# The decay sums of a state-space scan: which matrix is held and which is moved

## The chip, the cores and the metric

The kernel runs on one core of one Trainium2 chip. The metric is the device time of one execution in microseconds. Three runs of the kernel before took 1081.53, 1081.97 and 1082.54 us; the median is 1081.97 us. The names of the engines are those of the profile: PE is TensorE (matrix products), PEld its loading of the held operand, DVE is VectorE, ACT is ScalarE, POOL is GpSimd, and SP issues most of the DMAs.

## The reference, cut to what matters

The reference is a two-layer encoder over 256 tokens of width 1024. Each layer is a SwiGLU feed-forward block, a token mixer and a second feed-forward block, each followed by a layer norm, with shift, scale and gate computed from a condition vector. One of the two head groups of the mixer is a Mamba-2 scan with 8 heads. The part that the change touches is the decay between two tokens of a chunk:

```
a    = dt * A                                  # one number per token and head
a_cs = cumsum(a)                               # inside a chunk
seg  = a_cs[l] - a_cs[s]                       # sum of a over s < k <= l
decay = exp(where(s <= l, seg, -inf))
y_diag = einsum(C, B, decay, x * dt)
```

The kernel uses chunks of 128 tokens in place of 64, so there are two of them, t = 0 and t = 1. For each chunk and head it needs a 128 x 128 matrix of the sums of a over s < k <= l.

## The kernel before, in words

All weights are f32 in memory. ACT copies each piece into the format fp32r ("high"), DVE subtracts this copy from the original ("low"), and PE forms three products high·high, high·low and low·high. This is the bulk of PE's work. Weights come in pieces of 512 KB through a ring of 9 raw buffers; SP issues a load when a buffer's last reader (on DVE) is done. The pieces of the condition matrix (`ada`) go through the same ring, and DVE multiplies and adds them up without PE.

The high and low copies, and most intermediate tiles of the mixer, share one pool of 26 slots of 4 KB per partition, called `w` (function `wtile`). PSUM tiles of the mixer come from `mps` (two banks), `gps` (two banks) and `apt` (four banks).

The order of the work inside the mixer follows the list `MIX`. It gives the program order and so the priority; the order of the instructions on each engine is then fixed at build time by a list scheduler with a cost model of its own, which lets a later operation go first where an earlier one isn't ready in its reckoning. On the chip each engine runs its instructions in this fixed order. Only in the crossing from one block to the next is the order written out by hand. In every profile line the operations on PE, DVE and ACT carry L105, the line of the recording helper, so they are told apart by tile names. An x in a name stands for the mixer.

The steps of `MIX` around the change, in their order, are: `xe 0` and `xe 1` (the causal convolution of x: ACT `ca`, three steps on DVE, ACT `th`, DVE `xcx`, four times), `am t` (function `seg_pre`), `st` (one piece of the stream), `v 0` (24 x 2 products `ov`), `ta 0` (transposes `paT`), `seg t` (products `pse`, then `mt` = exp), `sg t` (DVE: `mt` times the matrix `gm`), `tx t` (transposes `pxs` of x), `v 1`, `av`, `y t` (products `pd`), `z 0`, `z 1` (products `oz`), then the output projection `p` (products `acc`, weights `w2`, `w3`, `w0`, `w1`).

The decay sums: `tri[k, l]` is 1 where l >= k, and `gtm[k, s]` is 1 where k > s. For each head ACT scales `gtm` by the column of a (`am`, eight activations of 128 x 128 for one t), and PE forms the product of the held `am` and the moved `tri` into a quarter of a PSUM bank; four heads fill a bank, and one ACT instruction takes the exponential of the whole bank. Both operands are f32.

Of the kernel before, what the change touches and what calls it, by code (L numbers as in the profile page):

```python
# [11 lines left out]
F32 = mybir.dt.float32  # L12
F32R = mybir.dt.float32r
BF16 = mybir.dt.bfloat16
I32 = mybir.dt.int32
AF = mybir.ActivationFunctionType
# [4 lines left out]
P = 128  # L21
# [11 lines left out]
HEADS = 8  # L33
# [33 lines left out]
def kernel(  # L67
# [24 lines left out]
    G = nc.gpsimd  # L92
# [19 lines left out]
    V, S, PE = Queue(nc.vector), Queue(nc.scalar), Queue(nc.tensor)  # L112
# [9 lines left out]
    cp = ctx.enter_context(tc.tile_pool(name="cp", bufs=1))  # L122
# [4 lines left out]
    sm = ctx.enter_context(tc.tile_pool(name="sm", bufs=3))  # L127
# [4 lines left out]
    def wtile(shape, name, dt=F32):  # L132
        return wp.tile([P] + list(shape), dt, tag="w", name=name)

    def mps(name):
        return pms.tile([P, 512], F32, tag="ms", name=name)
# [10 lines left out]
    def f(ap):  # L147
        return ap.bitcast(F32)
# [6 lines left out]
    def split(src, hi, lo):  # L155
        S.copy(hi, src)
        V.tensor_tensor(lo, src, f(hi), op=ALU.subtract)
# [6 lines left out]
    tri = cp.tile([P, P], F32, name="tri")  # L164
    G.affine_select(out=tri, in_=ones, compare_op=ALU.is_ge, fill=0.0, base=0,
                    pattern=[[1, P]], channel_multiplier=-1)
    gtm = cp.tile([P, P], F32, name="gtm")
    G.affine_select(out=gtm, in_=ones, compare_op=ALU.is_gt, fill=0.0, base=0,
                    pattern=[[-1, P]], channel_multiplier=1)
    neghalf = cp.tile([P, 16], F32, name="neghalf")  # L170
    G.memset(neghalf, -0.5)

# [781 lines left out]
    def mixer(mx_, nxt):  # L954
        l, qk, nm = mx_.l, mx_.qk, mx_.nm
# [69 lines left out]
        aa = sm.tile(bcs, F32, tag="aa", name="aa" + nm, bufs=1)  # L1025
# [180 lines left out]
        ssd = {}  # L1206

        def seg_pre(t):
            am = wtile([HEADS, P], f"am{nm}_{t}")
            for h in range(HEADS):  # L1210
                S.activation(am[:, h, :], gtm, AF.Identity, scale=aa[:, t, h:h + 1])
            ssd[t] = am

        def seg(t):
            am = ssd[t]
            mt = wtile([HEADS, P], f"mt{nm}_{t}")
            for g in range(2):
                ps = mps(f"pse{nm}_{t}{g}")
                for h in range(4):
                    PE.matmul(ps[:, h * P:(h + 1) * P], lhsT=am[:, 4 * g + h, :], rhs=tri, start=True, stop=True)  # L1220
                S.activation(mt[:, 4 * g:4 * g + 4, :], ps.rearrange("p (h k) -> p h k", h=4), AF.Exp)
            ssd[t] = mt

# [83 lines left out]
        def v_copy(t):  # L1307
# [3 lines left out]
        ops = dict(qk=mx_.proj, ev=mx_.evac, small=small, rope=rope, tqk=turn_qk, st=step,  # L1311
                   dt=lambda: held.update(dt=dt_mm()), dtf=lambda: dt_finish(*held.pop("dt")),
                   xm=xbc_mm, xe=xbc_evac, sc=scores_mm, sm=softmax, cums=cums, gram=gram, am=seg_pre,
                   cb=combine, ta=turn_a, seg=seg, sg=seg_mul, v=lambda t: tok_mm("v", t), vc=v_copy, tx=turn_x,
                   y=y_mm, av=lambda t: av(t, vt), z=lambda t: tok_mm("z", t), carry=carry, flush=flush,
                   gz=gate_z, pre=lambda: step(PRE), tf=to_feature, p=proj, up=upto_, rows=lambda: held.update(rows=ln_rows(l, s)))
# [9 lines left out]
    for l in range(DEPTH):  # L1326
        m, g = ms[l], gs[l]
# [41 lines left out]
```

## Time and profile before

| what | value |
|---|---|
| median of 3 runs | 1081.97 us |
| the profiled execution | 1082.18 us |
| its span, first to last instruction | 1080.3 us |
| mean granted TensorE clock | 0.984 |
| instructions on PE | 7433 |

The profile is one execution; its span is the time between the first and the last instruction, and the profiled execution took 1.88 us more than that. The granted clock is given in parts of full speed. Rows of a timeline give the start in us, the duration in us, the engine, and what is written from what; "[idle before <-releaser]" is the time that the engine stood idle before the instruction and what ended it. Matmuls are pipelined: the duration of one is longer than the distance between the starts of two, and it is the distance that counts for a sum.

### The profile page before, as it was taken

Reading aid. Unit: us, or ns where it says so; the run is one execution under the profiler, and the core shown is the slowest. Engines: PE = TensorE matmul, PEld = TensorE weight load, DVE = VectorE, ACT = ScalarE, POOL = GpSimd, SP = SyncE. Lnnn points to the kernel's source line nnn. Section 1 sums busy time; section 2 is a strip of 40 time slices with the busy share of each in tenths; the row PEclk is TensorE's granted clock in tenths of the full one; section 3 lists DMA queues with packets and bytes.
Section 4 is the critical chain, followed back from the end, with each engine's and each line's share of the span. In section 5 each row is a group of like instructions: output and inputs, shape, how many; then the busy total and the mean of one; then the engine's idle time right before and its main releaser. Section 6 shows DMA issues by size and latency. Waiting matters only on the chain.

```text
span 1080.3 us, 18994 instructions
## 1 busy us (share of the span) xinstructions
PE 1035.6 (96%) x7433; PEld 950.9 (88%) x7433; DVE 835.1 (77%) x1310; ACT 553.1 (51%) x946; POOL 53.0 (5%) x93
## 2 busy tenths in 40 slices
PE   4999999999997999999999999999999989999996
PEld 2799999989895899999988999998989979999995
DVE  5788688689988898769489768856999888756454
ACT  3475344476654664434466434546566567435241
POOL 1000000020010200000010000000100120000000
PEclk8999999999998999999999999999999999999999
DMA  9989888838368398789637889784664738776411
GB/s 343 311 301 383 292 291 313 295 114 270 100 202 281 120 307 306 293 323 328 237 117 259 302 317 362 277 288 126 174 212 141 230 101 304 247 241 214 161 40 39
DMA packets 162557, 258.24 MB, mean 239 GB/s; under 512 B 10806, under 2 KB 125982, under 8 KB 162468
## 3 DMA queue, kind: packets, MB, share of 16 engines
q1 hardware_dynamic: 162468, 257.04, 69.4%
q8 instruction: 58, 0.95, 0.3%
q14 instruction: 31, 0.25, 0.1%
HBM read 255.96 MB, written 1.05 MB: 238 GB/s over the span
## 4 chain that ended last, share of the span: by engine, by line
PE 77%; DVE 11%; ACT 6%; DMA 2%; issue 2%; POOL 1%; SPq 0%; DVEq 0%; POOLq 0%; ACTq 0%
PE ob L105 37%; PE acc L105 18%; PE oa L105 6%; PE oqkx L105 5%; PE accx L105 3%; PE ocx L105 2%; DVE xs L105 1%; PE ovx L105 1%; DVE ada L105 1%; DVE acc L105 1%; DVE cax L105 1%; PE pr L105 1%; ACT um L105 1%; ACT junk L105 1%; DVE lu L105 1%
## 5 line engine op out<-in xcount | busy, mean ns | idle before, releaser
L105 PE MATMUL ob<-uH,hg 128*128 128x256 f32 x576 | 163.1, 283 | 0.0
L105 PE MATMUL ob<-uL,hg 128*128 128x256 f32 x576 | 162.4, 282 | 0.0
L105 PE MATMUL ob<-uH,lg 128*128 128x256 f32 x576 | 161.8, 281 | 0.0
L105 PE MATMUL ob<-uH,hu 128*128 128x256 f32 x576 | 161.7, 281 | 0.0
L105 PE MATMUL ob<-uH,lu 128*128 128x256 f32 x576 | 161.7, 281 | 0.0
L105 PE MATMUL ob<-uL,hu 128*128 128x256 f32 x576 | 161.7, 281 | 0.0
L105 PE MATMUL acc<-ho,hH 128*128 128x512 f32 x352 | 137.5, 392 | 0.2 <-ACT hH L105 0.2
L105 PE MATMUL acc<-lo,hH 128*128 128x512 f32 x352 | 137.3, 390 | 0.0
L105 PE MATMUL acc<-ho,hL 128*128 128x512 f32 x352 | 137.2, 391 | 0.0
L105 ACT ACTIVATE sgb<-ob 128x256 f32<-128x256 f32 x72 | 27.6, 383 | 213.9 <-PE ob L105 213.3
L105 DVE TENSOR_TENSOR lo<-raw_o,ho 128x1024 fp32r<-128x1024 f32 x88 | 105.9, 1221 | 13.4 <-PE ob L105 6.5
L105 PEld LDWEIGHTS ob<-uH,hg 128*128 128x128 f32 x576 | 108.3, 188 | 7.8 <-issue 3.7
L105 PEld LDWEIGHTS ob<-uH,lg 128*128 128x128 f32 x576 | 110.2, 191 | 0.1
L105 PEld LDWEIGHTS ob<-uL,hg 128*128 128x128 f32 x576 | 108.2, 188 | 2.3
L105 PEld LDWEIGHTS ob<-uH,lu 128*128 128x128 f32 x576 | 110.2, 191 | 0.0
L105 DVE TENSOR_TENSOR lg<-raw_g,hg 128x1024 fp32r<-128x1024 f32 x84 | 100.6, 1221 | 11.5 <-ACT hg L105 6.1
L105 PEld LDWEIGHTS ob<-uH,hu 128*128 128x128 f32 x576 | 108.5, 188 | 0.0
L105 PEld LDWEIGHTS ob<-uL,hu 128*128 128x128 f32 x576 | 108.1, 188 | 0.0
L105 DVE TENSOR_TENSOR hfb<-ob,sgb 128x256 f32<-128x256 f32 x72 | 30.4, 422 | 94.4 <-ACT sgb L105 94.2
L105 DVE TENSOR_TENSOR lu<-raw_u,hu 128x1024 fp32r<-128x1024 f32 x84 | 100.6, 1220 | 3.5 <-ACT hu L105 1.9
L105 ACT CAST hg<-raw_g 128x1024 fp32r<-128x1024 f32 x84 | 86.3, 1050 | 32.0 <-PE acc L105 18.2
L105 ACT CAST ho<-raw_o 128x1024 fp32r<-128x1024 f32 x88 | 90.2, 1049 | 10.5 <-PE ob L105 9.0
(537 smaller groups left out, 2263.5 us busy)
## 6 DMA issues: line engine op xcount, KB each, us to landing
raw_o<-in_w_ffn_out_dram SPq DMA_DIRECT2D x88, 512.0 KB, 6.0
raw_g<-in_w_ffn_in_dram SPq DMA_DIRECT2D x84, 512.0 KB, 5.7
raw_u<-in_w_ffn_in_dram SPq DMA_DIRECT2D x84, 512.0 KB, 5.9
raw<-in_w_ffn_in_dram SPq DMA_DIRECT2D x8, 512.0 KB, 8.1
lg<-in_ln_g_dram SPq DMA_DIRECT2D x6, 512.0 KB, 6.2
lb<-in_ln_b_dram SPq DMA_DIRECT2D x6, 512.0 KB
raw_qk0x<-in_w_in_dram SPq DMA_DIRECT2D x4, 512.0 KB, 7.8
raw_qk1x<-in_w_in_dram SPq DMA_DIRECT2D x4, 512.0 KB
```

Of the source, the lines that this page charges most:

```text
L105: ins = emit(*args, **kwargs)
```

## The change

The roles of the two matrices are exchanged. The constant `gtm`, in an fp32r copy `gtmr` made once at the start on POOL, is now the held operand. The scaled matrix is now `tri` times a; it is made twice, from the high and the low part of a, as fp32r, and it is the moved operand. Since the held operand is the same for all heads, one product takes four heads (512 columns) at a time, and two products (high, low) add up in one bank. The column of a is split by one ACT copy and one DVE subtraction per t. There are now sixteen activations per t, and two tiles of the pool `w` where there was one.

```diff
+    gtmr = cp.tile([P, P], F32R, name="gtmr")
+    G.tensor_copy(gtmr, gtm)
...
         def seg_pre(t):
-            am = wtile([HEADS, P], f"am{nm}_{t}")
+            ssd[t] = am = [wtile([HEADS, P], f"am{e}{nm}_{t}", F32R) for e in "hl"]
+            ah = sm.tile([P, HEADS], F32R, tag="ah", name=f"ah{nm}_{t}", bufs=2)
+            al = sm.tile([P, HEADS], F32, tag="al", name=f"al{nm}_{t}", bufs=2)
+            split(aa[:, t, :], ah, al)
             for h in range(HEADS):
-                S.activation(am[:, h, :], gtm, AF.Identity, scale=aa[:, t, h:h + 1])
-            ssd[t] = am
+                S.activation(am[0][:, h, :], tri, AF.Identity, scale=f(ah)[:, h:h + 1])
+                S.activation(am[1][:, h, :], tri, AF.Identity, scale=al[:, h:h + 1])

         def seg(t):
...
-                for h in range(4):
-                    PE.matmul(ps[:, h * P:(h + 1) * P], lhsT=am[:, 4 * g + h, :], rhs=tri, start=True, stop=True)
+                for e in range(2):
+                    PE.matmul(ps, lhsT=gtmr, rhs=am[e][:, 4 * g:4 * g + 4, :], start=(e == 0), stop=(e == 1))
                 S.activation(mt[:, 4 * g:4 * g + 4, :], ps.rearrange("p (h k) -> p h k", h=4), AF.Exp)
```

## Rows read from the trace of the kernel before

**Rows 1.** The page's first part: busy us, share of the span, instructions of three engines.

```profile
PE 1035.6 (96%) x7433; PEld 950.9 (88%) x7433; DVE 835.1 (77%) x1310; ACT 553.1 (51%) x946; POOL 53.0 (5%) x93
```

**Rows 2.** Stretches (start:end, length, busy us by engine, clock), layer 0 then 1.

```profile
318.00:345.00 27.00, 20.33 (x120) 15.72 (x119) 22.62 (x32) 11.51 (x29) 4.16 (x3) 0.81 0.84 286
822.00:838.00 16.00, 15.71 (x135) 15.26 (x134) 14.99 (x24) 11.41 (x31) 0.68 (x1) 1.00 0.64 210
838.00:879.00 41.00, 40.58 (x252) 34.94 (x251) 35.08 (x62) 22.98 (x46) 4.85 (x10) 1.00 0.61 197
```

**Rows 3.** Timeline of PE in layer 1, the decay sums of t = 1.

```profile
830.94 1.12 PE L105 MATMUL psex<-tri,amx 128*128 128x128 f32 x8
831.82 0.36 PE L105 MATMUL ovx<-hv1x,uH 128*128 128x256 f32 x1
...
832.25 1.05 PE L105 MATMUL psex<-tri,amx 128*128 128x128 f32 x8
833.15 0.60 PE L105 MATMUL paTx<-ident,prx 128*128 128x128 f32 x4
833.50 0.36 PE L105 MATMUL ozx<-hz0x,uH 128*128 128x256 f32 x1
```

**Rows 4.** Timeline of PE in layer 1, two fp32r products of 512 columns.

```profile
853.28 0.39 PE L105 MATMUL accx<-lw2x,uH 128*128 128x512 f32 x1
853.51 0.40 PE L105 MATMUL accx<-hw2x,uH 128*128 128x512 f32 x1
```

**Rows 5.** Timeline of ACT in layer 1, around the scaled matrices.

```profile
814.88 2.16 ACT L105 ACTIVATE amx<-gtm,aax 128x128 f32<-128x128 f32 x7 [0.44 <-PE ocx L105]
...
817.55 0.55 ACT L105 ACTIVATE cax<-ocx,cvx 128x256 f32<-128x256 f32 x1
822.26 0.42 ACT L105 ACTIVATE thx<-cax 128x256 f32<-128x256 f32 x1 [4.16 <-DVE cax L105]
...
827.36 0.42 ACT L105 ACTIVATE thx<-cax 128x256 f32<-128x256 f32 x1 [1.91 <-DVE cax L105]
827.68 2.44 ACT L105 ACTIVATE amx<-gtm,aax 128x128 f32<-128x128 f32 x8
832.10 0.60 ACT L105 ACTIVATE mtx<-psex 128x512 f32<-128x512 f32 x1 [1.98 <-PE psex L105]
```

**Rows 6.** Timeline of PE in layer 0, after the decay sums.

```profile
326.25 2.07 PE L105 MATMUL pdx<-xdx,mtx 128*128 128x64 f32 x16 [1.88 <-DVE yc11x L105]
...
332.71 1.08 PE L105 MATMUL pr<-ada,ones 128*32 128x256 f32 x8 [3.00 <-DVE uL L105]
...
335.16 0.63 PE L105 MATMUL accx<-lw2x,uH 128*128 128x512 f32 x1
335.59 0.63 PE L105 MATMUL accx<-hw2x,uL 128*128 128x512 f32 x1
```

**Rows 7.** Timeline of DVE in layer 0, the stream.

```profile
307.63 1.28 DVE L105 SCALAR_TENSOR_TENSOR ada<-raw_(0, 5, 3)_1_3208,cT,ada 128x1024 f32<-128x1024 f32 x1
...
315.28 1.23 DVE L105 TENSOR_TENSOR lw2x<-raw_w2x,hw2x 128x1024 fp32r<-128x1024 f32 x1 [1.45 <-ACT hw2x L105]
```

**Rows 8.** Timeline of SP, the load that follows.

```profile
308.94 3.92 SPq L203 DMA_DIRECT2D raw_w2x<-in_w_out_dram  x2
```

**Rows 9.** Groups by form: names, shapes, count, busy us, mean ns, idle before.

```profile
L105 PE MATMUL psex<-tri,amx 128*128 128x128 f32 x64 | 8.8, 280 | 0.5 <-ACT aTx L105 0.5
L105 ACT ACTIVATE amx<-gtm,aax 128x128 f32<-128x128 f32 x32 | 10.0, 388 | 0.8 <-PE ocx L105 0.8
L105 DVE SCALAR_TENSOR_TENSOR ddx<-ddx,dz2x 128x16 f32<-128x16 f32 x14 | 2.4, 169 | 0.1
L168 POOL TENSOR_SCALAR_AFFINE_SELECT gtm<-ones 128x128 f32<-128x128 f32 x1 | 0.3, 292 | 0.0
```

**Rows 10.** Stretch of half clock in layer 0 (columns as in rows 2).

```profile
328.00:338.00 10.00, 7.00 (x24) 4.50 (x23) 10.00 (x11) 2.12 (x3) 0.00 (x0) 0.50 0.90 298
```

## The prediction, made before the changed kernel ran

> **What bounds the kernel now.** I read the shares of the engines first: PE is busy 96% of the span, DVE 77%, ACT 51% [rows 1]. That says PE bounds the whole; it doesn't say that PE bounds the stretch of the change. So I read the two mixers by stretches. In layer 1 PE is busy for 15.71 of 16 us while the decay sums are made, and for 40.58 of 41 us from there to the end of the output projection, at full clock [rows 2]. There PE's own work is the path: what it saves early, it has at the end. In layer 0 the stretch after the decay sums looks different: PE is busy 20.33 of 27 us at a mean clock of 0.81, DVE 22.62 [rows 2]. PE waits 1.88 us and 3.00 us there, both times for DVE [rows 6]. DVE is held in turn by the stream of weights: the last piece of one condition chunk is used up at 307.63 + 1.28 us, SP can then issue the load of w2 at 308.94, and DVE stands idle for 1.45 us before the first piece of w2 at 315.28 [rows 7, 8]. So in layer 0 a lead of PE ends in a longer wait for DVE. The same step of the same mixer is worth something in one layer and little in the other.
>
> **PE: what goes and what comes.** The 64 psex instructions of the trace are 32 f32 products (2 chunks, 2 layers, 8 heads), each recorded as two [rows 9]. Their 8.8 us of busy time is not the price, since they overlap; the distance of starts is. The group at 830.94 gives way to the next operation at 831.82, the one at 832.25 at 833.15: 0.88 and 0.90 us for four heads [rows 3]. Eight groups cost 8 x 0.89 = 7.1 us. In their place come two fp32r products of 512 columns per group. The trace has that form in accx: starts at 853.28 and 853.51, 0.23 us apart [rows 4]. Eight groups at 2 x 0.23 = 0.46 us cost 3.7 us. PE saves 7.1 - 3.7 = 3.4 us, 1.7 us in each layer. Bounds: a lone product shows 0.39 us [rows 4], so a group may take 0.23 + 0.39 = 0.62 us and PE save only 2.2 us in all; at best the products vanish behind others and the saving is the whole 7.1 us. I take 3.4 us, because the accx rows are the same form, back to back.
>
> The Trainium skill has other prices for a stream of products ("TensorE: Matmul & The Clock Gate", Back-to-back issue gap): about 81 ns for 128 columns and 131 ns for 512, sustained. By these a group would go from 0.65 to 0.26 us and PE would save 3.1 us. The rows say 0.11 and 0.23 us for the two forms, so here the trace differs, and it decides.
>
> **ACT: sixteen activations for eight.** One am takes 388 ns alone [rows 9]; eight in a row take 2.44 us [rows 5], so each further one costs (2.44 - 0.39) / 7 = 0.29 us. Eight more per chunk are 2.35 us, four chunks 9.4 us. That the output is fp32r and the input tri in place of gtm I cost at nothing: same shape, same function. Cover: after the am of t = 0 ACT does one ca and then idles 4.16 us; after the am of t = 1 it idles 1.98 us until PE is done [rows 5]. So 2.35 us fits behind the first for ACT itself, and only 2.0 of it behind the second. But ca at 817.55 stands behind the am, and three DVE steps wait for it. It comes about 2.35 us later. DVE has other work of the stream to put there (pieces of ada, 1.28 us each [rows 7]), so I expect DVE to stay busy in another order.
>
> **Who waits for the late am.** In layer 1 the am of t = 1 starts at 827.68. With high and low in turn, the first four heads are ready after 8 activations (830.1), all after 16: 827.68 + 15 x 0.29 + 0.39 = 832.4. PE would reach the second group at 832.25 less what it has saved by then (two groups of t = 0 and one of t = 1, 3 x 0.43 = 1.3 us), 830.95. It would be 1.5 us early. Whether it stands or works then depends on the fixed order: the products of z 0 are at hand, and PE already takes some at 833.50 [rows 3]. I take most of the gap as filled and charge 0.25 us in layer 1 for what isn't, splits included.
>
> **Small edits.** The split of a is one ACT copy and one DVE subtraction of 128 x 8 per chunk; the nearest row is 169 ns for 128 x 16 on DVE [rows 9], the am with 388 ns is the upper end for ACT. That is 0.17 to 0.4 us per engine and chunk, beside other work, as a is ready long before. The copy gtmr on POOL is near the 0.29 us of the select that makes gtm [rows 9], at the start, where the first products wait for DMAs; nothing. The second tile of am: the first waits 0.44 us for a product of ocx [rows 5], that is for a slot of a weight block just used. The high and the low half of this block have the same last readers, so two slots come free together; I cost the second at nothing. If it came only when the run of am was over, it would be 2.16 us late [rows 5], inside the 4.16 us of idle time.
>
> **The sum.** Layer 1: -1.7 + 0.25 = -1.45 us. Layer 0: PE's -1.7 us runs into the wait for DVE, 0. The profiled execution took 1082.18 us (span 1080.3 and 1.88 around it), so it would take 1080.7 us; it lies 0.21 us above the median of the runs, so on the scale of the medians I forecast 1080.5 us. About 0.2% (2.2 us) is what a measurement of this kernel can tell from no change, so this is "the same".
>
> **Rivals.**
> B, slower: PE stands behind the late am in both layers. The place is the second group of t = 1. If ca is 2.35 us late and the convolution steps follow it, the th before the am of t = 1 (827.36 [rows 5]) is late by the same, the am starts at 830.0 and ends at 834.8. PE starts the group 2.5 us later than now, and has only this group's 0.43 us still to gain: +2.1 us per layer. It decides from the point at which the lateness of ACT passes what PE has ready to fill with. One layer gives 1084.1, both 1086.2. A longer pause can also cost clock: in layer 0, after PE's 1.88 us wait, the granted clock is 0.50, the lower of the two levels, from 328 to 338 us [rows 6, 10], and accx starts are 0.43 us apart in place of 0.23 [rows 4, 6]; the 24 instructions there at 0.2 us are 4.8 us, up to 1091. For it speaks that ACT's work here doubles and that the order isn't made from chip times; against it that ACT is busy only 11.41 of 16 us [rows 2] and that z 0 is at hand. The Trainium skill ("TensorE: Matmul & The Clock Gate", What happens when you issue a matmul) says that only weight loads are pulled ahead and products stay in program order; by that rule a product that waits for am holds all of z 0 behind it. Rows 6 agree, PE stands 3.00 us in one place.
> C, faster: while the convolution is late, DVE takes the pieces of ada earlier, the load of w2 goes out earlier, and DVE's 1.45 us before w2 goes [rows 7]. Then layer 0 gains too: -1.45 - 1.45 = -2.9 us, 1079.1; with part of the half-clock stretch gone (up to 4.8 us) down to 1075. For it: every wait of layer 0 hangs on this stream. Against: it needs the order to change in just this way.
> D: the saving of PE ends in waits in both layers, because DVE is nearly full in layer 1 as well (35.08 of 41 us [rows 2]): 1081.9, within 0.3 us of now.
>
> **How the numbers follow.** Forecast 0.45, with its own range from 1079.0 (all of 3.4 us) to 1082; B 0.25; C 0.24; D 0.06. Faster by over 0.2%, below 1079.8: C, most of it (0.22), and the lower tail of the forecast (0.08), 0.30. Slower, above 1084.1: B, 0.25. Within: 0.45. The range leaves out the clock tails of B (0.10) and C (0.08): 1077.8 to 1086.0.
>
> **What would show it.** Right: psex as 16 instructions in all, groups 0.46 us apart at full clock, 64 scaled activations on ACT at 0.29 us, and in layer 1 the last accx before the crossing about 1.5 us earlier than the end of the 838 to 879 stretch. Wrong: an idle PE over 1 us before psex with ACT as releaser (B); w2 of layer 0 issued before 308 us and a shorter wait before lw2 (C); products of psex 0.4 us apart; or the stretch 318 to 345 with another clock than 0.81, which would move the time by more than all the terms above.

## The result, and the profile after

The changed kernel takes 1089.12 us (median of 4 runs, 1087.45 to 1090.69); the kernel before took 1082.26 us beside it. The ratio is 1.0061 [1.0047, 1.0075]: slower by 6.6 us, where 1080.5 was forecast. The profiled execution took 1089.77 us, with a span of 1088.1 us. The mean granted clock of the four runs was 0.979 to 0.987, against 0.984 in the profile before: on the whole the clock isn't what is lost.

The first part of the page after, against [rows 1]:

```profile
PE 1029.7 (95%) x7385; PEld 943.3 (87%) x7385; DVE 836.5 (77%) x1314; ACT 562.8 (52%) x982; POOL 52.5 (5%) x94
```

ACT is busy 9.7 us more, where 9.4 were reckoned, and PE 5.9 us less (its busy time; the saving was reckoned from the starts). So the work came out about as priced and the time went the other way: what grew is waiting.

Two events that every kernel has tell where. SP's load of the convolution's weights marks the start of a mixer, the first `ob` product the start of the block after it.

| stretch | before, us | after, us | difference |
|---|---|---|---|
| to the start of mixer 0 | 240.28 | 240.55 | +0.3 |
| mixer 0 to the next block | 156.43 | 158.46 | +2.0 |
| two blocks between | 371.78 | 371.98 | +0.2 |
| mixer 1 to the next block | 144.91 | 148.84 | +3.9 |
| last block to the end of the span | 166.9 | 168.3 | +1.4 |

The mixers hold 6.0 of the 7.8 us. The last block isn't touched by the change: in the 19 profiles of this study it takes 166.9 to 167.4 us or, in five of them, 168.2 to 168.3, with no tie to what was edited; I leave it out.

The same three stretches as in [rows 2], after:

```profile
318.00:345.00 27.00, 17.63 (x100) 13.88 (x99) 24.92 (x33) 11.34 (x24) 2.71 (x2) 0.75 0.80 262
822.00:838.00 16.00, 15.33 (x126) 14.75 (x125) 15.32 (x22) 8.77 (x25) 0.00 (x0) 1.00 0.73 245
838.00:879.00 41.00, 37.46 (x234) 31.74 (x233) 31.74 (x53) 24.92 (x54) 3.61 (x5) 1.00 0.53 175
```

In the third stretch PE falls from 40.58 to 37.46 of 41 us and DVE from 35.08 to 31.74: both stand more. (The times are the same, but mixer 1 starts 2.5 us later here; from 840.5 to 881.5 us the two are 37.46 and 32.87.)

ACT of layer 1, the answer to [rows 5] (the mixer starts at 770.99 here, at 768.49 before):

```profile
821.62 0.54 ACT L105 ACTIVATE cax<-ocx,cvx 128x256 f32<-128x256 f32 x1
827.16 0.42 ACT L105 ACTIVATE thx<-cax 128x256 f32<-128x256 f32 x1 [1.27 <-DVE cax L105]
827.49 0.55 ACT L105 ACTIVATE cax<-ocx,cvx 128x256 f32<-128x256 f32 x1
832.30 0.42 ACT L105 ACTIVATE thx<-cax 128x256 f32<-128x256 f32 x1
832.62 0.39 ACT L105 ACTIVATE amhx<-tri,ahx 128x128 fp32r<-128x128 f32 x1
...
837.02 0.39 ACT L105 ACTIVATE amlx<-tri,alx 128x128 fp32r<-128x128 f32 x1
838.88 0.60 ACT L105 ACTIVATE mtx<-psex 128x512 f32<-128x512 f32 x1 [1.48 <-PE psex L105]
841.16 0.60 ACT L105 ACTIVATE mtx<-psex 128x512 f32<-128x512 f32 x1 [1.68 <-PE psex L105]
```

Counted from the mixer's start, the third `ca` comes at 50.6 us (before 49.1), the fourth at 56.5 (54.1), the activations of t = 1 end at 66.4 (61.6), and the second `mt` of t = 1 starts at 70.2 (64.9). The lateness grows at each step: 1.5, 2.4, 4.8, 5.3 us. In layer 0 the second `mt` is 6.1 us late (70.9 for 64.8).

PE of layer 1 at these products, the answer to [rows 3]:

```profile
838.10 0.40 PE L105 MATMUL psex<-amhx,gtmr 128*128 128x512 f32 x1
838.33 0.28 PE L105 MATMUL ozx<-lz1x,uH 128*128 128x256 f32 x1
838.45 0.39 PE L105 MATMUL psex<-amlx,gtmr 128*128 128x512 f32 x1
...
840.38 0.39 PE L105 MATMUL psex<-amhx,gtmr 128*128 128x512 f32 x1
840.61 0.28 PE L105 MATMUL ozx<-hz0x,uL 128*128 128x256 f32 x1
840.73 0.39 PE L105 MATMUL psex<-amlx,gtmr 128*128 128x512 f32 x1
```

PE doesn't stand. Its fixed order has the products of z first: all operands of the second group are there at 837.4, and it starts at 840.38 behind the 15 `oz` that follow the first group.

DVE stands. Before, in layer 0, it met both `mt` of t = 1 without idle time and had pieces of `ada` to put between:

```profile
305.23 0.69 DVE L105 TENSOR_TENSOR mtx<-mtx,gmx 128x512 f32<-128x512 f32 x1
305.83 1.28 DVE L105 SCALAR_TENSOR_TENSOR ada<-raw_(0, 5, 3)_0_3136,cT,ada 128x1024 f32<-128x1024 f32 x1
307.03 0.69 DVE L105 TENSOR_TENSOR mtx<-mtx,gmx 128x512 f32<-128x512 f32 x1
```

After, layer 0 and then layer 1:

```profile
303.98 1.28 DVE L105 SCALAR_TENSOR_TENSOR ada<-raw_(0, 5, 3)_1_3210,cT,ada 128x1024 f32<-128x1024 f32 x1
...
309.76 0.69 DVE L105 TENSOR_TENSOR mtx<-mtx,gmx 128x512 f32<-128x512 f32 x1 [2.12 <-ACT mtx L105]
312.04 0.69 DVE L105 TENSOR_TENSOR mtx<-mtx,gmx 128x512 f32<-128x512 f32 x1 [1.59 <-ACT mtx L105]
312.65 0.74 DVE L105 TENSOR_SCALAR ada<-raw_(0, 7, 0)_0_3216,cT 128x1024 f32<-128x1024 f32 x1
...
839.51 0.69 DVE L105 TENSOR_TENSOR mtx<-mtx,gmx 128x512 f32<-128x512 f32 x1 [2.19 <-ACT mtx L105]
841.79 0.69 DVE L105 TENSOR_TENSOR mtx<-mtx,gmx 128x512 f32<-128x512 f32 x1 [1.59 <-ACT mtx L105]
...
868.84 0.88 DVE L105 SCALAR_TENSOR_TENSOR yc10x<-yv1x,ryx,snwx 128x256 f32<-128x256 f32 x2 [0.87 <-POOL ryx L181]
```

It waits 3.7 and 3.8 us for `mt`. The last piece of the condition chunk, which came behind both `mt` before [rows 7], is used up ahead of them; in layer 0 a piece of the next chunk stands behind them that had been at hand for long (SP had issued the one after it at 292.26). Not all of this wait is new time: summed from 40 us after the mixer's start to DVE's last step of y (`yc10`), DVE's waits are 8.4 us for 4.7 in layer 1, but 8.6 for 7.8 in layer 0, where others are gone, the 1.45 us before w2 [rows 7] among them. PE pays later: its waits after that, layer 0 (the answer to [rows 6]) and layer 1:

```profile
335.71 1.08 PE L105 MATMUL pr<-ada,ones 128*32 128x256 f32 x8 [5.82 <-DVE uL L105]
...
853.90 0.50 PE L105 MATMUL accx<-hw2x,uH 128*128 128x512 f32 x1 [1.99 <-ACT uH L105]
884.90 1.09 PE L105 MATMUL ptp<-ident,xn 128*128 128x128 f32 x8 [1.28 <-DVE xn L105]
887.77 3.56 PE L105 MATMUL oa<-hg,uH 128*128 128x256 f32 x16 [1.78 <-ACT uH L105]
```

And the clock, in stretches of 4 us of the crossing in layer 1 (columns as in [rows 2]):

```profile
883.00:887.00 4.00, 1.71 (x11) 1.02 (x9) 3.24 (x8) 2.63 (x7) 0.58 (x1) 1.00 0.40 131
887.00:891.00 4.00, 3.23 (x15) 3.23 (x16) 3.96 (x11) 3.19 (x7) 0.59 (x1) 0.57 0.00 0
```

After a stretch in which PE was busy 1.71 of 4 us the granted clock falls to 0.57, that is, to the lower level for most of it. The sixteen `oa` products there take 3.40 us from their first start to the next row's, for 2.00 us before (882.01 to 884.01): 1.4 us are lost. From 40 us after the start of mixer 1, PE's waits sum to 7.5 us, for 3.3 before; 4.2 + 1.4 for the clock - 1.7 of saved products = 3.9, as measured. This is the account of one execution: the kernel with the convolution moved, below, loses as much clock in layer 1 (0.988 over the mixer, for 0.989 here) and is not slow.

### The profile page after: what moved, and what is told of

It reads as the page before. It is cut to its first block, busy times and chain, and to the rows that moved or that the text cites. A ratio compares the mean times of both kernels' runs of the same rounds, so it can differ in the third digit from the quotient of the medians.

```text
span 1088.1 us, 18938 instructions
## 1 busy us (share of the span) xinstructions
PE 1029.7 (95%) x7385; PEld 943.3 (87%) x7385; DVE 836.5 (77%) x1314; ACT 562.8 (52%) x982; POOL 52.5 (5%) x94
## 4 chain that ended last, share of the span: by engine, by line
PE 77%; DVE 12%; DMA 3%; ACT 3%; issue 2%; POOL 2%; SPq 0%; DVEq 0%; POOLq 0%; ACTq 0%
PE ob L105 37%; PE acc L105 21%; PE oa L105 4%; PE ocx L105 2%; PE accx L105 2%; PE ovx L105 2%; DMA raw_g<-in_w_ffn_in_dram 2%; PE ozx L105 2%; DVE xs L105 1%; PE oqkx L105 1%; POOL rmp L181 1%; POOL rp L181 1%; PE pr L105 1%; DVE acc L105 1%; DVE lu L105 1%
```

## The experiments

Each ratio is to the kernel before, in runs on the same chip. The theory to begin with: the doubled activations delay the third `ca`, and this lateness reaches the second `mt` and DVE. The rival: the loss is in the new products and operands.

**High part only.**

```diff
-                S.activation(am[1][:, h, :], tri, AF.Identity, scale=al[:, h:h + 1])
...
-                for e in range(2):
-                    PE.matmul(ps, lhsT=gtmr, rhs=am[e][:, 4 * g:4 * g + 4, :], start=(e == 0), stop=(e == 1))
+                PE.matmul(ps, lhsT=gtmr, rhs=am[0][:, 4 * g:4 * g + 4, :], start=True, stop=True)
```

> The changed kernel with the low part left out: eight scaled activations per chunk and one product per group of four heads (the decay sums have the precision of the high part only). Theory 1, the doubled work on ACT makes the change slow: with eight activations the convolution's ca and th come no later than before (ca of the third column block within 0.5 us of its place before), DVE doesn't stand for mt (under 0.5 us), and the time is 1079 to 1082.5, that is, before or a little faster. Rival 2, the exchange of the held and the moved matrix itself makes it slow (the products of four heads at a time, fp32r): 1086 to 1090 as in the changed kernel. Rival 3, any other order of the scheduler costs some us: anything from 1083 to 1090 with no more wait for mt on DVE.

Measured: 1079.82 us, ratio 0.9993 [0.9982, 1.0003]. With eight activations the exchange costs nothing; the loss hangs on the other eight, or on the second product of each group, which is left out with them. The next two runs part these.

**Sixteen activations, old products.**

```diff
                 S.activation(am[:, h, :], gtm, AF.Identity, scale=aa[:, t, h:h + 1])
+                S.activation(an[:, h, :], tri, AF.Identity, scale=aa[:, t, h:h + 1])
```

> The kernel before, with eight more activations of 128x128 per chunk into a second tile that nothing reads; the products are the f32 products of before. Theory 1 (ACT): as slow as the changed kernel or slower, since the 3.4 us of products that it saves are not saved here: 1088 to 1093; DVE stands over 2 us in each layer before it multiplies mt of the second chunk. Rival 2 (the products): 1081.5 to 1083, as before. Rival 3: slower, but with the wait elsewhere.

Measured: 1084.78 us, ratio 1.0042 [1.0029, 1.0055]: slower without any new product, as expected, but by 4.5 us where 7 to 12 were expected. DVE stands in the same place, here in layer 1:

```profile
835.41 0.69 DVE L105 TENSOR_TENSOR mtx<-mtx,gmx 128x512 f32<-128x512 f32 x1 [1.71 <-ACT mtx L105]
837.73 0.69 DVE L105 TENSOR_TENSOR mtx<-mtx,gmx 128x512 f32<-128x512 f32 x1 [1.63 <-ACT mtx L105]
```

**The convolution ahead of the activations.** In MIX, `xe 1` (the third and fourth `ca`) stands behind `am 0`, not ahead of it as the list of steps above has it. Here it is moved ahead, in the changed kernel:

```diff
-"...xm 1,am 0,v 0,st 2,xe 1,ta 0..."
+"...xm 1,v 0,st 2,xe 1,am 0,ta 0..."
```

> The changed kernel with the convolution step xe 1 ahead of am 0 in the list of priorities; all sixteen activations stay. Theory 1, in the form that the activations delay the convolution and only by that the second chunk: ca of the third block is back within 1 us of its place before, th of the fourth within 1 us, am of the second chunk starts 3 us sooner than in the changed kernel and the time falls to 1083 to 1086. If the sixteen activations in themselves are what is too long: still 1087 to 1090. Rival 2: 1087 to 1090.

Measured: 1079.32 us, ratio 0.9989 [0.998, 0.9998]. All sixteen activations and the products are there, and the whole loss is gone, more than the 1083 to 1086 expected. ACT and DVE of layer 0 (the mixer starts at 241.09):

```profile
289.39 0.55 ACT L105 ACTIVATE cax<-ocx,cvx 128x256 f32<-128x256 f32 x1
...
304.89 0.60 ACT L105 ACTIVATE mtx<-psex 128x512 f32<-128x512 f32 x1 [0.53 <-PE psex L105]
307.18 0.60 ACT L105 ACTIVATE mtx<-psex 128x512 f32<-128x512 f32 x1 [1.20 <-PE psex L105]
```
```profile
307.33 0.69 DVE L105 TENSOR_TENSOR mtx<-mtx,gmx 128x512 f32<-128x512 f32 x1
307.94 1.28 DVE L105 SCALAR_TENSOR_TENSOR ada<-raw_(0, 5, 3)_1_3210,cT,ada 128x1024 f32<-128x1024 f32 x1
309.13 0.69 DVE L105 TENSOR_TENSOR mtx<-mtx,gmx 128x512 f32<-128x512 f32 x1
```

The third `ca` now stands between the activations; DVE meets both `mt` without idle time.

**Both scaled matrices on POOL.** Two multiplications of 128 x 1024 per chunk in place of sixteen activations.

```diff
-            for h in range(HEADS): ...
+            for e, c in enumerate((f(ah), al)):
+                G.tensor_tensor(am[e], tri.unsqueeze(1).broadcast_to([P, HEADS, P]),
+                                c.unsqueeze(2).broadcast_to([P, HEADS, P]), op=ALU.mult)
```

> The changed kernel with both scaled tiles made by POOL in one instruction each (triangle broadcast over heads times a broadcast over columns, 128x1024), none on ACT. POOL is 5% busy. Theory 1: ACT has 2.35 us less per chunk than in the kernel before; if a POOL instruction takes under 4 us, the products of the second chunk are no later than before and the time is 1078 to 1081.5, faster than before by PE's 3.4 us or a part. Rival 2: 1086 to 1090. If POOL needs over 6 us an instruction, or slows DVE by sharing its path to memory, the group of the first chunk waits for it: 1084 to 1090 with POOL as releaser of psex, or longer DVE instructions beside it.

Measured: 1088.54 us, ratio 1.0078 [1.0065, 1.0091]. What the rows show beside it, POOL and DVE holding each other up, stands in the last section.

**Control: the same move in the kernel before.** Edit as in the run with the convolution ahead.

> The kernel before with the same move in the list MIX as in the last run but one: `xe 1` (the third and fourth block of the convolution) ahead of `am 0`. It has eight activations and the old products. Theory (what the changed kernel lost is the place of the convolution's steps behind the doubled activations; the exchange itself saves PE time): here only 2.4 us of activations stood ahead of the third `ca`, so the move brings at most 1 us, 1080 to 1082, and it stays 1 to 3 us above the changed kernel with the move (1079.3), which has PE's saving. Rival (the move is a better order by itself and the exchange is worth nothing): 1079.3 within 1 us, no difference to the changed kernel with the move.

Measured: 1081.43 us, ratio 0.9999 [0.9987, 1.0011]. The move alone is worth nothing; in the changed kernel it is worth 1.0061 - 0.9989, about 8 us.

**The move, sixteen activations, old products.**

> The kernel before with `xe 1` ahead of `am 0` and with eight unread activations more per chunk. Theory (the eight activations cost only through what stands behind them): within 1 us of the run above, so 1080 to 1082.5, and the two `mt` of the second chunk are no longer waited for by DVE. Rival (the time on ACT costs by itself): as without the move, 1084 to 1086, with DVE waiting 3 us per layer for `mt`.

Measured: 1079.14 us, ratio 0.9975 [0.9965, 0.9984]: the activations cost nothing once `ca` isn't behind them. That it is faster than the control by 2.6 us, with eight unread activations more per chunk, was not expected. The list scheduler sees other costs and orders the work otherwise; in the profiles layer 0 is 1.6 us shorter (154.9 for 156.5), but its granted clock is also 0.989 for 0.945, and which of the two brings this isn't shown. So what an edit brings by the way is as large as the gain that was forecast.

**DVE's stand filled.**

```diff
-                V.tensor_tensor(mg, mg, gm..., op=ALU.mult)
+                ins = V.tensor_tensor(mg, mg, gm..., op=ALU.mult)
+                if t == 1:
+                    order(ins, stream["v"])     # and in MIX: st 1,st 1,st 1,sg 1,z 0
```

> The changed kernel with one difference on DVE: the two multiplications of the second `mt` by `gm` are ordered behind the first two pieces of the second condition chunk of the stream (0.75 and 1.28 us), which had landed long before and stood behind them; the convolution stays as late as in the changed kernel. Theory (the loss has two parts, the late convolution and DVE's stand behind a late `mt`): the two pieces fill 2.0 of the 3.7 us per layer, so 1 to 2 us come back per layer, 1085 to 1087.5. Rival 1 (DVE's idle time is only a symptom, the chain through the late convolution sets the end): 1089 within 1 us. Rival 2 (the stand is the whole loss): 1081 to 1083.

Measured: 1090.05 us, ratio 1.0081 [1.0062, 1.0099]. Nothing came back; it is close to the number of rival 1, by which DVE's idle time is a symptom of the late chain. DVE in layer 0:

```profile
306.84 1.28 DVE L105 SCALAR_TENSOR_TENSOR ada<-raw_(0, 7, 0)_1_3330,cT,ada 128x1024 f32<-128x1024 f32 x1
308.34 0.69 DVE L105 TENSOR_TENSOR mtx<-mtx,gmx 128x512 f32<-128x512 f32 x1 [0.21 <-ACT mtx L105]
310.70 0.69 DVE L105 TENSOR_TENSOR mtx<-mtx,gmx 128x512 f32<-128x512 f32 x1 [1.67 <-ACT mtx L105]
314.02 0.16 DVE L105 SCALAR_TENSOR_TENSOR sox<-sox,epx 128x4 f32<-128x4 f32 x1 [2.63 <-ACT sqo0x L105]
```

The first wait went from 2.12 to 0.21, and a new one of 2.63 us stands behind: what DVE does next is late too. (In layer 1 the next pieces of the stream are those of w2, so there the multiplication came later still; the test holds for layer 0 only.)

**The low half on DVE.** With the move; one DVE multiplication of 128 x 1024 for the low half.

> The changed kernel with `xe 1` ahead of `am 0`, and with the low scaled matrix of all eight heads made by one DVE multiplication of 128 x 1024 (the nearest rows are 1.23 us) in place of eight activations. Theory (with the convolution out of the way the activations on ACT cost nothing, and DVE is the fuller engine in this stretch): 1079.5 to 1082, no better than with all sixteen on ACT (1079.3). Rival (the activations still delay the second `mt`): 1077 to 1078.5.

Measured: 1085.13 us, ratio 1.0034 [1.002, 1.0048]: worse than either side expected. It lasts 1.21 us as reckoned; what it does to DVE the table below shows.

**Which chunk's activations.** The low half and its product left out for one t; the edit for t = 0, its activations:

```diff
-                S.activation(am[1][:, h, :], tri, AF.Identity, scale=al[:, h:h + 1])
+                if t != 0:
+                    S.activation(am[1][:, h, :], tri, AF.Identity, scale=al[:, h:h + 1])
```

> The changed kernel, but for the first chunk (t = 0) the low scaled matrix is left out: eight activations and one product per group there, sixteen and two for t = 1. Theory (the loss begins with the third `ca` of the convolution, which stands behind the activations of t = 0, and the lateness runs through `th` to the activations and `mt` of t = 1): most of the 7 us comes back, 1080 to 1082.5, the first `mt` of t = 1 in layer 0 starts before 306 us. Rival (the sixteen activations of t = 1 just ahead of the products and `mt` are what delays): 1086 to 1089, `mt` after 308 us.

Measured: 1080.1 us, ratio 0.9998 [0.9985, 1.001], the first `mt` of t = 1 at 304.35, as the theory had it.

> The changed kernel, but for the second chunk (t = 1) the low scaled matrix is left out: sixteen activations for t = 0, eight for t = 1. Theory (the activations of t = 0 carry the loss): at most a third comes back, since `mt` of t = 1 is earlier by the 2.35 us of eight activations at best, 1085 to 1088. Rival (the activations of t = 1 carry it): 1080 to 1082.5.

Measured: 1083.17 us, ratio 1.0022 [1.0012, 1.0032]. The theory gave it a third of the loss at most, it brings some 60%. So the two halves don't add: t = 0's eight alone cost 1.0022 - 0.9993, 3 us; t = 1's alone under 1 us; together 7. One reading is that lateness costs little until it has used up what the order has to spare; as the gap of some 3.5 us isn't far above the 2.6 us that an edit brought by the way, it isn't shown.

**The products twice.** With the move.

```diff
-                for e in range(2):
+                for e in (0, 1, 0, 1):
```

> The changed kernel with `xe 1` ahead of `am 0`, and each pair of products (high, low) is issued twice, the second pair over the first: PE gets 8 groups x 0.46 us = 3.7 us of work more, about the 3.4 us that the exchange saves. Theory (PE's saving counts in layer 1 and ends in waits for DVE in layer 0): in layer 1 the last accx is 1.8 us later against the mixer's start than with single products (107.3 us), in layer 0 nothing is lost; 1079 to 1081. Rival 1 (PE's time counts in both layers): 1083. Rival 2 (it counts in none, the fixed order alone decides): layer 1 unchanged at 107.3 us, 1078 to 1079.5.

Measured: 1082.9 us, ratio 1.0014 [1.0005, 1.0022]: 2.7 us above the same kernel with single products, for 3.7 us of work; the time is rival 1's. In the profiles the next block begins 1.7 us later in layer 1 (144.9 for 143.2) and at the same time in layer 0 (155.9 for 156.0 us after the mixer's start), which is the theory's split; the last accx of layer 1, which the theory named, comes 3.2 us later (110.5 for 107.3), not 1.8. Rival 2 falls, unless the order alone moved that much. In layer 1, then, work on PE counts.

**A try at the stream.** With the move, two `st 1` moved from ahead of `tx 0` and `v 1` to behind `up z1`.

> A try for a faster version: the changed kernel with `xe 1` ahead of `am 0` and with two steps of the stream moved from ahead of `tx 0` and `v 1` to behind `z 1`, by which the first low piece of w2 in layer 0 comes after two pieces of the second condition chunk on DVE, not after four. Theory (layer 0 ends with this stream: in the run with sixteen activations and the old products, whose order has w2 as early, layer 0 is 1.1 us shorter than in the changed kernel with the move): 1077.5 to 1079. Rival (the place of w2 in DVE's order is not what made layer 0 shorter there): 1079 to 1081.

Measured: 1082.3 us, ratio 1.0008 [1.0, 1.0017]: slower than without, though the first low piece of w2 came 2.0 us earlier (77.2 for 79.2 us after the mixer's start): that place alone doesn't make layer 0 shorter.

**The attention ahead of the late products.** In MIX of the changed kernel:

```diff
-"st 1,tx 0,am 1,cb 1,seg 1,st 1,v 1,vc 1,ta 1,st 1,av 0,y 0,st 1,sg 1,z 0,carry,gz 0,av 1,z 1..."
+"st 1,tx 0,cb 1,st 1,v 1,vc 1,ta 1,av 0,av 1,am 1,seg 1,st 1,y 0,st 1,sg 1,z 0,carry,gz 0,z 1..."
```

> The changed kernel with the rest of the attention (`ta 1`, `av 0`, `av 1`: transposes paT, products pox) and `v 1` ahead of `am 1` and `seg 1` in MIX. The convolution, the sixteen activations and the second `mt` stay as late as in the changed kernel (70 us after the mixer's start) or later. Theory (the late psex costs mostly because paT and pox of the attention stand behind it in PE's fixed order, and their branch, aT, sqo0x, yc01x, uH, is what the first accx waits for): most of the 7 us comes back, 1081 to 1084. Rival (the cost comes through `mt` itself, that is through y 1 and the gate of t = 1): 1088 to 1091.

Measured: 1090.2 us, ratio 1.0081 [1.0068, 1.0094]. The rival's number: the attention's products queued behind psex are not what costs.

> Both moves in the changed kernel: `xe 1` ahead of `am 0`, and the attention ahead of `am 1`. A try for a faster version. Theory of the run above: the attention's branch is out of the way of both, but `mt` comes as late as 68 us; 1078 to 1081. Rival: `mt` of t = 1 sets the end, so later than with the first move alone (1079.3): 1082 to 1085.

Measured (both moves): 1084.74 us, ratio 1.0032 [1.0019, 1.0044]; again the rival's.

> Control: the kernel before with the attention ahead of `am 1`. Theory: there psex of t = 1 isn't late and the move brings little, 1080 to 1083. Rival (the order with the attention first is better by itself): 1076 to 1079.

Measured (the control): 1084.13 us, ratio 1.0022 [1.0014, 1.0031], slower than expected: in this order the second `mt` is late in the kernel before as well, by 9 us, and that costs 2.4 us, far less than in the changed kernel. So the lateness of `mt` by itself isn't the measure either.

**What goes with the time.** I then laid the profiles beside each other by one more event: `yc10`, DVE's last step of y for t = 1, behind which the last transposes and the last quarter of the output projection stand. Layer 1, us after the mixer's start; idle is the sum of DVE's waits of over 0.15 us from 40 us after the start to `yc10`:

| kernel | ratio | second mt | DVE idle | yc10 | next block |
|---|---|---|---|---|---|
| before | 1 | 64.9 | 4.7 | 93.6 | 144.9 |
| move alone | 0.9999 | 63.3 | 4.2 | 92.8 | 144.3 |
| move, 16 activations, old products | 0.9975 | 65.6 | 4.2 | 93.1 | 144.4 |
| changed, with the move | 0.9989 | 65.2 | 3.6 | 92.9 | 143.2 |
| high part only | 0.9993 | 63.8 | 3.8 | 92.2 | 142.4 |
| low half left out for t = 1 | 1.0022 | 68.0 | 6.3 | 95.7 | 146.1 |
| attention first, kernel before | 1.0022 | 74.2 | 7.2 | 96.1 | 147.3 |
| 16 activations, old products | 1.0042 | 69.7 | 8.4 | 97.7 | 147.1 |
| **changed** | 1.0061 | 70.2 | 8.4 | 97.9 | 148.8 |
| attention first, changed | 1.0081 | 78.3 | 10.6 | 101.4 | 151.2 |
| move, low half on DVE | 1.0034 | 66.5 | 6.6 | 98.0 | 147.4 |
| both on POOL | 1.0078 | 68.2 | 5.7 | 98.9 | 148.4 |

The next block begins 49.4 to 51.5 us after `yc10`, in every row (in layer 0, 51.4 to 53.2 us in all 19 profiles). And `yc10` less the idle time is 88.4 to 89.5 us in nine rows; with the attention first in the changed kernel it is some 91, and in the two last rows, where DVE has more to do or is held up, 91.4 and 93.2. The second number says less than it seems: DVE works off its fixed order, so `yc10` less its idle time is just the work that the order puts ahead. What the table shows is that this work stayed nearly the same, and that a late `yc10` goes with idle time of DVE and makes the next block late. Whether DVE's own work is the path from the mixer's middle to `yc10` is another question. Two runs asked it:

```diff
+                V.tensor_tensor(mg, mg, gm..., op=ALU.mult)     # a second time; in the other run: none
```

> The changed kernel with `xe 1` ahead of `am 0` (1079.3), with every multiplication of `mt` by `gm` issued twice: DVE gets 4 x 0.6 = 2.4 us of work more per layer, none of it urgent, PE and ACT nothing. Theory (from the middle of the mixer to the second y of t = 1, `yc10`, DVE is the path in both layers; in all profiles so far the next block begins 49 to 53 us after `yc10`): `yc10` is 1.5 to 2.4 us later in each layer, 1081.5 to 1084.5. Rival (PE's work is the path in layer 1, as the prediction said, and DVE has room): 1079 to 1080.5.

Measured: 1083.04 us, ratio 1.0016 [1.0005, 1.0027]: 2.9 us more, as the theory has it. `yc10` of layer 1, which stood at 860.53 - 767.60 = 92.9 us after the mixer's start, comes at 865.72 - 770.62 = 95.1:

```profile
865.72 0.88 DVE L105 SCALAR_TENSOR_TENSOR yc10x<-yv1x,ryx,snwx 128x256 f32<-128x256 f32 x2 [0.88 <-POOL ryx L181]
```

> The same kernel with these multiplications left out (the mask by C and B is missing): DVE has 2.4 us of work less per layer. Theory (DVE is the path): `yc10` 1.5 to 2.4 us earlier in each layer, 1074.5 to 1077.5. Rival (PE is the path in layer 1): at most 1 us, 1078.5 to 1080.

Measured: 1081.62 us, ratio 1.0004 [0.9995, 1.0013]. A miss for both: nothing is gained, and 1.6 us are lost against the kernel with the multiplications, at the edge of the noise. The run is no clean test, as the order changed with it: on ACT the copy `vt1` now stands ahead of the activations of t = 1 and waits for PE, they end 66.2 us after the mixer's start in place of 62.5, and DVE stands where it had worked. ACT, then DVE, in layer 1:

```profile
828.42 0.59 ACT L105 COPY vt1x<-ovx 128x512 f32<-128x512 f32 x1 [2.69 <-PE ovx L105]
...
837.25 1.23 DVE L105 TENSOR_TENSOR lw2x<-raw_w2x,hw2x 128x1024 fp32r<-128x1024 f32 x1 [3.81 <-ACT hw2x L105]
```

So work added on DVE costs at once (2.4 us per layer made the next block of layer 1 2.4 us later, 145.6 for 143.2), and so did work added on PE in layer 1 (1.85 us made it 1.7 us later). That work taken off DVE would be gained isn't shown.

## Why the prediction was wrong

**The prices were right.** Sixteen psex rows, two products 0.23 us apart; the first two of layer 0:

```profile
294.34 0.39 PE L105 MATMUL psex<-amhx,gtmr 128*128 128x512 f32 x1
294.57 0.40 PE L105 MATMUL psex<-amlx,gtmr 128*128 128x512 f32 x1
```

The activations, by groups:

```profile
L105 ACT ACTIVATE amhx<-tri,ahx 128x128 fp32r<-128x128 f32 x32 | 12.4, 388 | 0.5 <-PE ocx L105 0.5
L105 ACT ACTIVATE amlx<-tri,alx 128x128 fp32r<-128x128 f32 x32 | 12.4, 387 | 0.0
```

64 of 0.39 us, 0.29 apart; ACT's busy time grew by 9.7 us, splits included, for 9.4 forecast; the copy gtmr took 0.29 us, the split 0.19 on ACT and 0.15 on DVE.

**The saving isn't shown.** With the same move in both, the changed kernel is at 0.9989 [0.998, 0.9998] and the old at 0.9999 [0.9987, 1.0011]: 1.1 us, where 1.45 were forecast, but the intervals overlap. By the profiles layer 1 begins its next block 1.0 us earlier and layer 0 0.5. The old products with the move and sixteen activations are at 0.9975, faster than the new ones. A saving of this size would fit and is smaller than what an edit brings by the way (2.6 us).

**The step that failed** is on ACT: "It comes about 2.35 us later. DVE has other work of the stream to put there (pieces of `ada`, 1.28 us each [rows 7]), so I expect DVE to stay busy in another order." The first sentence held (1.5 us in layer 1, 2.5 in layer 0), and DVE did take the pieces. That was cover used once: what it did early it no longer had when the next wait came. The lateness came back larger, at `mt` (5.3 us in layer 1, 6.1 in layer 0), since two `ca`, the second run of sixteen and the place of psex among the `oz` each added to it, and there DVE stood 3.7 us per layer. I followed the late `ca` for one wait, where there were three in a row. So the term for the late activations was put at 0.25 us in layer 1 ("I take most of the gap as filled and charge 0.25 us") and at nothing in layer 0; layer 1 lost 3.9 us where 1.45 were to be gained, and layer 0 lost 2.0. That the late `ca` begins the loss is shown by the runs with the convolution ahead and with the low half left out for t = 0. That DVE's stand at `mt` carries it on is argued from the rows: filling that stand in layer 0 brought nothing back.

**Behind it a reading that went too far.** "There PE's own work is the path", for layer 1 from PE's 40.58 of 41 us [rows 2]. That work on PE counts there, the doubled products bear out (1.7 us for 1.85). But it isn't the only path: the doubled multiplications count just as fully on DVE, which is busy 35.08 of 41 us in the same row, and a DVE that waits makes PE wait a dozen us later. Rival D had read DVE's row in this way, and priced it only as a saving that is lost.

**Rival B** had the place, and the size in part by luck. The activations of t = 1 end at 834.8 in its sum, 66.3 us after the mixer's start, and 66.4 was measured. But PE doesn't stand before psex, which B took as the cost; DVE stands after it, and PE's waits come a dozen us later. The second group of psex starts 5.6 us later (69.4 for 63.8 us after the mixer's start), not 2.5. That 1089.1 lies between B's 1086.2 and its 1091 with clock is chance: the clock fell anew in layer 1, in layer 0 it stayed as it was (0.957 for 0.956 over the mixer), it cost 1.4 us in the profile, and the mean clock of the runs isn't lower. The rule quoted with it, that of the Trainium skill ("TensorE: Matmul & The Clock Gate", What happens when you issue a matmul) that products stay in program order, agrees with the trace in the opposite sense: it was psex that stood behind `oz`, 840.38 for operands of 837.4. The range ended at 1086.0, below B's own sum for both layers.

**Rival C** saw rightly that the load of w2 goes out earlier: SP issues the first of its two parts at 305.28 for 308.94 [rows 8]. DVE's 1.45 us before w2 did go, as C said. It brought nothing, as DVE then stood for `mt`, and the first low piece of w2 came at 321.62 for 315.28.

**Open** are: how much of the loss is the order that the scheduler made for the doubled activations, and would be another with another order; why sixteen activations with the old products cost 4.5 us and not more than the changed kernel, which has PE's saving; why removing DVE's work gained only 0.8 us in layer 0 (155.2 for 156.0); and the two lengths of the last block.

## What to carry to other kernels

Added work on a half-idle engine is free only if nothing urgent stands behind it in that engine's fixed order: follow what stands behind through every hand-over until it meets a nearly full engine, and add the delays up; cover can be used once. A busy share near 100% doesn't make an engine the only path: here work added on either of two engines cost time. An event that keeps its distance to the end in all variants tells up to where the loss arose; what the engine waited for there still has to be followed. Where a scheduler fixes the order, any edit may reshuffle it by an amount (here 2.6 us) as large as a small change's gain, so run the same reordering on the old kernel before crediting the change, and look whether the order changed before reading an edit as a test.

## What the runs showed of the hardware

In these rows POOL and DVE shut each other out for whole instructions. Both matrices on POOL, layer 0, chunk t = 1; POOL, then DVE:

```profile
297.78 2.87 POOL L1216 TENSOR_TENSOR amhx<-tri,ahx 128x1024 fp32r<-128x1024 f32 x1 [4.85 <-PE psex L105]
300.61 2.87 POOL L1216 TENSOR_TENSOR amlx<-tri,alx 128x1024 fp32r<-128x1024 f32 x1
```
```profile
297.62 1.27 DVE L105 SCALAR_TENSOR_TENSOR ada<-raw_(0, 5, 1)_0_3098,cT,ada 128x1024 f32<-128x1024 f32 x1
298.81 0.47 DVE L105 SCALAR_TENSOR_TENSOR cax<-ocx,cvx,cax 128x255 f32<-128x255 f32 x1
299.20 2.52 DVE L105 SCALAR_TENSOR_TENSOR ada<-raw_(0, 5, 1)_1_3104,cT,ada 128x1024 f32<-128x1024 f32 x1
302.04 1.99 DVE L105 TENSOR_TENSOR mtx<-mtx,gmx 128x512 f32<-128x512 f32 x1
```

For t = 0 each POOL multiplication took 1.90 us, though there too a DVE step beside the second was held up (`xcx`, 1.64 for 0.42 us). Here the first begins while DVE's `ada` runs and takes 2.87; the next `ada` lasts 2.52 for 1.28 us and ends 1.1 us after POOL's first; `mt` times `gm` lasts 1.99 for 0.69 and ends 0.55 us after POOL's second. `cax`, which reads PSUM, keeps its 0.47. The Trainium skill ("SBUF — State Buffer", SBUF: two separate sides) says that these two engines share a port pair that one holds for its whole instruction while the other blocks, on DVE's side where it has two SBUF inputs; the rows agree. Some 3.8 us per layer of DVE's time (1.2 for t = 0, 1.2 and 1.3 here) went that way, near the 3.7 us by which the row of POOL stands out against the changed kernel in the table (93.2 for 89.5 us, `yc10` less idle).
